# Splitting the first load of a 2x nearest-neighbour upsampling over two DMA queues

## The chip, the cores and the metric

The kernel runs on one core of a Trainium2 chip. The metric is the device time of one execution in microseconds, the median of several runs. The profile that is quoted below was taken on one execution; its times count from the core's first recorded instruction that is shown, here the first DMA issue.

## The reference

The input is an array of 16 x 64 images of 64 x 64 float32 values. Each pixel is repeated twice along each axis, so that the output has images of 128 x 128. Nothing is computed: the output is four copies of every input value, in order.

```python
batch, channels, h, w = (16, 64, 64, 64)
...
for i in range(new_h):
    for j in range(new_w):
        src_i = i // scale_factor
        src_j = j // scale_factor
        result[:, :, i, j] = x[:, :, src_i, src_j].copy()
```

The input is 16.78 MB and the output 67.11 MB.

## The kernel before

The 65,536 image rows are laid over 128 partitions, 512 consecutive rows (R = 512) of 64 values each, so that a partition owns one contiguous stretch of the input (128 KB) and one of the output (512 KB). A single on-chip tile, `mem`, holds both the input (`xt`, its upper part) and the expanded rows (`u`), which are written alternately at the bottom of the tile and downwards from the end of input rows that have been used up.

The loads are three DMAs at L195, cut by `cuts`: rows 0 to 32 (`HEAD`, 8 KB of every partition, 1.05 MB), rows 32 to 288 (64 KB of every partition, 8.39 MB) and rows 288 to 512 (56 KB, 7.34 MB). SyncE issues all three.

The work then goes through nine groups of rows (`rows = [54, 38, 54, 60, 54, 62, 64, 62, 64]`). For each group VectorE copies its rows from `xt` into `u` with a broadcast that repeats each value and each row (L215), and one DMA (L217) stores `u` to the output. Group 0 is copied in two instructions: its first row alone (L214), then the other 53 (L215), which need the second load, since group 0 ends at row 54. SyncE issues the stores of groups 0, 1 and 8, ScalarE those of groups 2 to 7. The profile shows one DMA queue for each of the two issuing engines.

The order of instructions comes from the program and from semaphores that the framework places. Two functions change it by hand when the program is finished. `begin_before_barrier` takes the first `EARLY = 3` instructions of SyncE out of the program's body and puts them ahead of the opening barrier, in front of SyncE's drain, so that the loads are issued before the engines have met. `close_early` rebuilds the end of the program: the closing barrier is passed while the last store is still under way, GpSimd clears the semaphores, and SyncE alone waits for the last landing.

Of the kernel before, what the change touches and what calls it, by code (L numbers as in the profile page):

```python
# [6 lines left out]

EARLY = 3  # L10


def begin_before_barrier(nc):

    blocks = nc.main_func.blocks
    main, body = blocks[0], blocks[1]
    sp = mybir.EngineType.SP
    loads = [i for i in body.instructions if i.engine == sp][:EARLY]  # L20
    for load in loads:
        assert isinstance(load, mybir.InstDMACopy), type(load)
        assert not (load.sync_info and load.sync_info.on_wait)
    names = [i.name for i in loads]
    body.instructions = [i for i in body.instructions if i.name not in names]
    kept = list(main.instructions)
    at = next(
        n
        for n, i in enumerate(kept)
        if i.engine == sp and isinstance(i, mybir.InstDrain)  # L30
    )
    kept[at:at] = loads
    main.instructions = kept


def close_on_gpsimd(nc):
# [117 lines left out]
@with_exitstack  # L154
def kernel(
    ctx: ExitStack,
    tc: tile.TileContext,
    x: bass.AP,
    scale_factor: int,
    out: bass.AP,  # L160
):
    nc = tc.nc
    nc.at_finalize(begin_before_barrier)
    nc.at_finalize(close_early)
    P = nc.NUM_PARTITIONS
    s = int(scale_factor)
    B, C, H, W = x.shape
    R = B * C * H // P
    fdt = x.dtype

    xp = x.rearrange("b c h w -> (b c h) w").rearrange("(p r) w -> p r w", p=P)
    op = out.rearrange("b c (h hd) w -> (b c h) (hd w)", hd=s).rearrange(
        "(p r) w -> p r w", p=P
    )

    rows = [54, 38, 54, 60, 54, 62, 64, 62, 64]
    GROW = s * s
    FREE = 79
    WF = FREE * GROW * W
    assert sum(rows) == R
    mem_pool = ctx.enter_context(tc.tile_pool(name="mem", bufs=1))
    mem = mem_pool.tile([P, WF + R * W], fdt, name="mem")
    xt = mem[:, WF:].rearrange("p (r w) -> p r w", r=R)

    HEAD = 32
    cuts = [0, HEAD, R // 2 + HEAD, R]
    for lo, hi in zip(cuts, cuts[1:]):
        nc.sync.dma_start(out=xt[:, lo:hi], in_=xp[:, lo:hi])  # L195

    def expanded(r0, r1):
        return (
            xt[:, r0:r1].unsqueeze(2).unsqueeze(4).to_broadcast([P, r1 - r0, s, W, s])
        )  # L200

    r0 = 0
    before = (0, 0)
    for n, k in enumerate(rows):
        size = k * GROW * W
        at = 0 if n % 2 == 0 else WF + r0 * W - size
        assert at >= before[1] or at + size <= before[0]
        before = (at, at + size)
        u = mem[:, at : at + size].rearrange(
            "p (k a w b) -> p k a w b", k=k, a=s, w=W  # L210
        )
        k0 = 1 if n == 0 else 0
        if k0:
            nc.vector.tensor_copy(out=u[:, :k0], in_=expanded(r0, r0 + k0))  # L214
        nc.vector.tensor_copy(out=u[:, k0:], in_=expanded(r0 + k0, r0 + k))  # L215
        issuer = nc.sync if n in (0, 1, len(rows) - 1) else nc.scalar
        issuer.dma_start(out=op[:, r0 : r0 + k, :], in_=u)  # L217
        r0 += k
# [35 lines left out]
```

## Time and profile before

| What | Value |
|---|---|
| median of 3 runs | 197.12 us (197.11 to 197.22) |
| profiled execution: span | 195.7 us |
| profiled execution: own time | not listed apart from its span; the runs' median lies 1.4 us above it |
| VectorE busy | 76.9 us (39%) |
| DMA traffic | 83.89 MB in 1728 packets, mean 429 GB/s |
| DMA queue of SyncE / of ScalarE, share of 16 engines | 44.3% / 55.0% |
| chain that ended last | DMA 61%, VectorE 24% |

The span runs from the first DMA issue to the last instruction, which waits for the last store's landing. The table's share of a queue is the time that its packets took, as a share of the 16 DMA engines' time over the span; the two together are over 99%. In the tables by stretch a packet's bytes and its time are booked where the packet begins, so a short stretch can show more than a DMA engine can move, and the stretch after it nothing.

### The profile page before, as it was taken

How to read it: one execution, taken by the hardware profiler on the slowest of the kernel's cores; microseconds unless marked ns; L12 is line 12 of the kernel's file. 1: busy time of each engine (PE TensorE's matmuls, PEld its weight loads, DVE VectorE, ACT ScalarE, POOL GpSimd, SP SyncE). 2: the span in 40 equal slices, each digit the busy share in tenths (PEclk: the TensorE clock that was granted, in tenths of full speed). 3: DMA queues.
4: the chain of work that ended last, by engine and by line, in shares of the span. 5: the costliest groups of instructions: out<-in, count | busy, mean ns of one | idle time of the engine just before them, and what ended most of it. 6: DMA issues, size and time to landing. Idle time of an engine off the chain costs nothing.

```text
span 195.7 us, 76 instructions
## 1 busy us (share of the span) xinstructions
DVE 76.9 (39%) x10; POOL 0.2 (0%) x4
## 2 busy tenths in 40 slices
DVE  0000099990029287059008805920790079000000
POOL 0000000000000000000000000000000000000000
DMA  9999989989898988999999899999999999999994
GB/s 429 429 429 429 402 375 492 445 362 543 362 435 382 540 384 362 543 402 402 402 492 452 362 543 415 415 415 415 429 429 429 429 415 441 550 476 422 429 429 214
DMA packets 1728, 83.89 MB, mean 429 GB/s; under 512 B 192, under 2 KB 192, under 8 KB 192
## 3 DMA queue, kind: packets, MB, share of 16 engines
q10 hardware_dynamic: 864, 46.66, 55.0%
q1 hardware_dynamic: 864, 37.22, 44.3%
HBM read 16.78 MB, written 67.11 MB: 429 GB/s over the span
## 4 chain that ended last, share of the span: by engine, by line
DMA 61%; DVE 24%; SPq 0%; issue 0%
DMA out_dram<-mem 49%; DVE mem L215 24%; DMA mem<-in_x_dram 12%; SPq L195 0%
## 5 line engine op out<-in xcount | busy, mean ns | idle before, releaser
L215 DVE COPY mem<-mem 128x13824 f32<-128x13824 f32 (+5 forms) x9 | 76.6, 8515 | 84.6 <-DMA out_dram<-mem 65.5
L214 DVE COPY mem<-mem 128x256 f32<-128x256 f32 x1 | 0.3, 293 | 4.9 <-DMA mem<-in_x_dram 4.9
L235 POOL MEMSET const-bfloat16-1.0<- 128x1 bf16 x1 | 0.1, 101 | 0.0
L235 POOL MEMSET const-uint8-127<- 128x1 uint8 x1 | 0.1, 101 | 0.0
L235 POOL MEMSET const-float32-0.0<- 128x1 f32 x1 | 0.1, 98 | 0.2 <-issue 0.2
L235 POOL MEMSET const-float32-1.0<- 128x1 f32 x1 | 0.1, 98 | 0.0
## 6 DMA issues: line engine op xcount, KB each, us to landing
out_dram<-mem ACTq DMA_DIRECT2D x2, 7936.0 KB, 31.6
out_dram<-mem ACTq DMA_DIRECT2D x2, 6912.0 KB, 23.7
out_dram<-mem ACTq DMA_DIRECT2D x1, 7680.0 KB, 26.1
mem<-in_x_dram SPq DMA_DIRECT2D x1, 7168.0 KB, 40.2
out_dram<-mem SPq DMA_DIRECT2D x1, 6912.0 KB, 18.9
out_dram<-mem SPq DMA_DIRECT2D x1, 4864.0 KB, 25.1
mem<-in_x_dram SPq DMA_DIRECT2D x1, 1024.0 KB, 4.8
mem<-in_x_dram SPq DMA_DIRECT2D x1, 23.8
```

Of the source, the lines that this page charges most:

```text
L214: nc.vector.tensor_copy(out=u[:, :k0], in_=expanded(r0, r0 + k0))
L215: nc.vector.tensor_copy(out=u[:, k0:], in_=expanded(r0 + k0, r0 + k))
L235: nc = _bacc.Bacc("TRN2", target_bir_lowering=False, num_devices=1)
```

## The change

The first of the three loads, rows 0 to 32 of all 128 partitions, is replaced by two: partitions 0 to 63 issued by SyncE and partitions 64 to 127 issued by ScalarE. The other two loads stay as they are, on SyncE. `EARLY` becomes a table, and `begin_before_barrier` does for each engine in it what it did for SyncE: three DMA issues of SyncE and one of ScalarE are put ahead of the opening barrier. The copy at L214 has two landings to wait for instead of one.

```diff
-EARLY = 3
+EARLY = {mybir.EngineType.SP: 3, mybir.EngineType.Activation: 1}
...
-    sp = mybir.EngineType.SP
-    loads = [i for i in body.instructions if i.engine == sp][:EARLY]
...
+    for engine, count in EARLY.items():
+        loads = [i for i in body.instructions if i.engine == engine][:count]
...
+        at = next(
+            n
+            for n, i in enumerate(kept)
+            if i.engine == engine and isinstance(i, mybir.InstDrain)
+        )
+        kept[at:at] = loads
+        main.instructions = kept
...
     HEAD = 32
     cuts = [0, HEAD, R // 2 + HEAD, R]
-    for lo, hi in zip(cuts, cuts[1:]):
+    half = P // 2
+    nc.scalar.dma_start(out=xt[half:, :HEAD], in_=xp[half:, :HEAD])
+    nc.sync.dma_start(out=xt[:half, :HEAD], in_=xp[:half, :HEAD])
+    for lo, hi in zip(cuts[1:], cuts[2:]):
         nc.sync.dma_start(out=xt[:, lo:hi], in_=xp[:, lo:hi])
```

More of the change, by code (lines that the diff above doesn't have):

```diff
@@ L18, in begin_before_barrier @@
     main, body = blocks[0], blocks[1]
-    sp = mybir.EngineType.SP
-    loads = [i for i in body.instructions if i.engine == sp][:EARLY]
[L21 to L33, printed above, removed]
+    for engine, count in EARLY.items():
+        loads = [i for i in body.instructions if i.engine == engine][:count]
+        for load in loads:
+            assert isinstance(load, mybir.InstDMACopy), type(load)
+            assert not (load.sync_info and load.sync_info.on_wait)
+        names = [i.name for i in loads]
+        body.instructions = [i for i in body.instructions if i.name not in names]
+        kept = list(main.instructions)
+        at = next(
[5 more added lines that the diff above has]
+        main.instructions = kept
 def close_on_gpsimd(nc):
```

## The prediction

> **What bounds the kernel now.** I read the page first: the span, the DMA strip and the traffic; then the chain that ended last; then tables of busy time by stretch.
>
> ```profile
> span 195.7 us, 76 instructions
> DMA  9999989989898988999999899999999999999994
> HBM read 16.78 MB, written 67.11 MB: 429 GB/s over the span
> DMA packets 1728, 83.89 MB, mean 429 GB/s; under 512 B 192, under 2 KB 192, under 8 KB 192
> L215 DVE COPY mem<-mem 128x13824 f32<-128x13824 f32 (+5 forms) x9 | 76.6, 8515 | 84.6 <-DMA out_dram<-mem 65.5 <-DMA mem<-in_x_dram 19.1
> L214 DVE COPY mem<-mem 128x256 f32<-128x256 f32 x1 | 0.3, 293 | 4.9 <-DMA mem<-in_x_dram 4.9
> ```
>
> The strip cuts the span into 40 slices, and the DMA engines are at eight or nine tenths in all but the last. 16.78 + 67.11 = 83.89 MB go through in 195.7 us. Two stretches of steady work, one of loads and one of stores, give the rate (columns: stretch, length, VectorE, GpSimd, clock, DMA share, GB/s):
>
> ```profile
> 5.00:24.00 19.00, 0.15 (x1) 0.00 (x0) 1.00 1.00 435
> 157.00:187.00 30.00, 8.69 (x1) 0.00 (x0) 1.00 1.02 441
> ```
>
> At 435 GB/s 83.89 MB last 192.9 us. So 195.7 - 192.9 = 2.8 us is all that the span holds beside a full stream: its start and its last landing. VectorE is busy for 76.9 us (76.6 + 0.3) and waits on DMAs for the rest, so it is not the bound; the chain's early steps show how the work hands over.
>
> ```profile
> 21 pieces in order of time: start us, us, what
> 0.00 0.37 SPq L195
> 0.37 0.05 issue
> 0.42 23.76 DMA mem<-in_x_dram
> 24.19 0.02 issue
> 24.21 14.30 DVE mem L215
> 38.51 0.02 issue
> 38.52 18.93 DMA out_dram<-mem
> ...
> ```
>
> The chain starts with the second load (23.76 us from its issue), not the first. The first store is issued at 38.52 and takes 18.93 us to land at 57.45. Its size and the loads' landings say whether the stream ran dry there:
>
> ```profile
> L195 SPq DMA_DIRECT2D mem<-in_x_dram x3: 373/424/432, 0.0 to 0.9; - x3
> DMA to landing us min/median/max: 4.8/23.8/40.2
> out_dram<-mem SPq DMA_DIRECT2D x1, 6912.0 KB, 18.9
> ```
>
> 6912 KB are 7.08 MB, or 16.3 us at 435 GB/s; counted back from 57.45 the store's bytes began at about 41.2. The third load, issued at 0.9, landed 40.2 us later, at 41.1. The store stood 2.6 us in the queue behind it and there was no hole. So whatever the DMA engines lose or gain in the first microseconds reaches the end in full, and nothing later takes it up or adds to it.
>
> **The first load, close up.** The first 5 us in 40 slices of 0.125 us: share of the DMA engines, and GB/s, where a packet's bytes stand where it begins. Below it, whole microseconds of the table by stretch.
>
> ```profile
> DMA  0000000099330023699999999999979999990000
> GB/s 0 0 0 0 0 0 0 0 393 590 66 66 0 0 66 131 262 393 393 393 459 459 393 459 393 393 459 393 524 328 393 524 852 2753 2622 2622 0 0 0 0
> ```
>
> ```profile
> 4.00:5.00 1.00, 0.14 (x1) 0.00 (x0) 1.00 2.56 1106
> 5.00:6.00 1.00, 0.15 (x1) 0.00 (x0) 1.00 0.00 0
> 6.00:7.00 1.00, 0.00 (x0) 0.00 (x0) 1.00 2.42 1049
> 7.00:8.00 1.00, 0.00 (x0) 0.00 (x0) 1.00 0.00 0
> 8.00:9.00 1.00, 0.00 (x0) 0.00 (x0) 1.00 0.30 131
> 9.00:10.00 1.00, 0.00 (x0) 0.00 (x0) 1.00 2.12 918
> ```
>
> Three things. First packets begin 1.0 us after the issue (eight empty slices), and the flow is steady from about slice 16, 2.0 us. From there 0.125 us carries about 410 GB/s until slice 32, where the large packets of the second load follow with no empty slice between: the handover from one DMA to the next costs nothing that can be seen. And the sixteen engines walk nearly in step: 1049 GB/s over 1 us is 1.05 MB, sixteen packets of 64 KB, that is one packet of every engine begun between 6 and 7 us, none between 5 and 6 or 7 and 8. The large packets first begin in four slices (852 to 2622), so the engines lie within 0.5 us of one another.
>
> **The change, part by part.** The load of 1.05 MB (128 partitions of 8 KB, eight packets an engine) becomes two of 0.52 MB. I assume that each spreads over all sixteen engines, four packets of 8 KB each.
>
> Issue. ScalarE gains one DMA issue, SyncE keeps three. Rows:
>
> ```profile
> L217 ACTq DMA_DIRECT2D out_dram<-mem x6: 338/339/376, 64.9 to 146.9; - x6
> L235 ACTq DRAIN x1: 8/8/8, 0.1 to 0.1; - x1
> L235 SPq DRAIN x1: 125/125/125, 1.4 to 1.4; - x1
> ```
>
> ScalarE reaches the barrier at 0.1 us and SyncE at 1.4, so ScalarE's 0.34 to 0.38 us are over by 0.5, a microsecond ahead of the barrier: no cost, and if that cover were gone VectorE still has nothing to do until 4.9. SyncE's first issue, 0.37 us for 128 partitions, may shrink; if it went by partitions the loads behind it would leave 0.19 us sooner. A sooner start is worth something only for the first packets: between 0 and -0.2; I take -0.1, the middle, since the 0.34 us store issue and the 0.37 us load issue differ little with size.
>
> Waits. The copy at L214 now waits for two landings. It is followed by 19 us of idle time before the large copy at L215, which hangs on the second load (24.21), so even a first load that lands at 12 us, its upper packets alternating with three 64 KB packets of 2.4 us, costs nothing. Completion marks: the 192 packets under 512 B are sixteen for each of the twelve DMAs, so a thirteenth adds sixteen; the slices around the handover put their price at 0. The later stores wait for one more semaphore that came 20 us earlier, and sit in a queue anyway (2.6 us at the tightest place worked out above): 0.
>
> The transfer itself. No row of this trace shows a transfer over 64 partitions. Bounds: if the sixteen engines are the limit, 1.05 MB last 2.41 us as now, change 0. If the side of the on-chip memory is the limit and 64 partitions give half of it, a stretch in which all engines are in one half goes at half rate: 4.82 us, +2.41. Loads and stores both run at 435 to 441 GB/s though one reads and the other writes the outer memory, so the limit is in what they share, engines or on-chip side; this does not tell which. I take the upper region, nearest to the in-step rows: SyncE's packets reach every engine first, ScalarE's come some 0.1 us behind, so all sixteen engines want the lower half at the same moment, then all the upper. It is not the whole 2.41, because engines that are apart miss each other. For two engines that share a way in, a packet of 0.30 us (2.41/8) takes 0.60 - d when they are d apart. Over a spread of 0.5 us two engines are 0.17 us apart on average: 8 x 0.13 = 1.0 us. But the end waits for the slowest engine, which is in one of the closest pairs; I choose d = 0.075, a quarter packet: 8 x 0.225 = 1.8 us.
>
> [...]
>
> Sum: -0.1 + 0 + 0 + 1.8 = +1.7 us. The profiled span of 195.7 becomes 197.4. The runs' median is 197.12, 1.4 above the span, for what lies around it and is not touched: 198.8.
>
> **Rivals.**
> (a) The halves cost nothing: the engines are the limit, or half of them are soon in the upper half while the others are in the lower. For it: after the start the spread (0.5 us) is more than a packet (0.30), so some pairs are out of step already. Against it: it needs all eight pairs out of step, as the slowest one sets the end. Price 0 to -0.2 from the issue and 0.2 of leftover collisions: 196.9 to 197.3, centre 197.0.
> (b) Faster: the two queues ramp up side by side. The strip shows 1.0 us from 1.0 to 2.0 in which sixteen first packets are on their way and little follows. If a second queue's packets travel in that time, a part is saved: at most 1.0 less one packet's own 0.30, 0.7 us, together with the -0.1 of the issue 196.3; half of it 196.7. It decides over (a) when over 0.3 us of the ramp goes, with no collision. Against it: after the ramp packets already flow at the full rate in a single queue, so their way is already overlapped, and a ramp that two queues share has the same first arrival.
> (c) The change does not do what it says: the upper half starves behind the second load. Then its four packets an engine are met by large packets of other engines, and both sides pay: up to 8 x 0.30 = 2.4 us, 199.5; more if the second load's landing slips past its cover of 1.6 us (2.6 in the queue less 1.0 from issue to first packet).
>
> **How the numbers follow.** Forecast, collisions with 0.9 to 2.5 us lost: 198.0 to 199.6, chance 0.62. Rival (a) 0.24. Rival (b) 0.10. Rival (c) with more than 2.5 us lost 0.04; its smaller losses are in the forecast. About 0.2%, 0.39 us, is what a measurement of this kernel can tell from no change: the forecast and (c) lie above it, (a) within, (b) below. So faster 0.10, same 0.24, slower 0.66. The time is that of the forecast, 198.8, whose own range is 198.0 to 199.6. It holds 0.62 alone, so the range reaches down over (a) to 196.9, and to 199.6 above: 0.86, with (b) and the rest of (c) left out.
>
> **What would show it.** Right: in the first 5 us the slices from 2.0 on carry well under 410 GB/s, some near 200; the large packets begin about 1.5 to 2.2 us later than slice 32 and spread over more than 0.5 us; the large copy at the second load's landing starts near 25.9 instead of 24.21, and all later copies are as late. ScalarE's load stands near 0.1 us and SyncE's first issue is 0.2 to 0.37 us. Wrong: the slices keep 410 GB/s and the large copy starts within 0.3 us of 24.21 (rival a), or sooner (b). A landing of the second load that is late while the end is not would overthrow the first part, that early losses reach the end in full.

## The result and the profile after

The changed kernel takes 199.58 us (199.45 to 199.68), before 197.12 us: ratio 1.0119, 95% interval 1.0107 to 1.0131. It is 2.46 us slower; 198.8 had been forecast. Run once more beside the last experiments it took 199.23 us against 197.20 (1.0100, 1.0086 to 1.0113), so the loss is 2.0 to 2.5 us.

The page of the changed kernel (VectorE's copies stand at L217 and L218 now):

```profile
span 198.2 us, 80 instructions
HBM read 16.78 MB, written 67.11 MB: 423 GB/s over the span
L218 DVE COPY mem<-mem 128x13824 f32<-128x13824 f32 (+5 forms) x9 | 76.6, 8515 | 84.4 <-DMA out_dram<-mem 65.5
L217 DVE COPY mem<-mem 128x256 f32<-128x256 f32 x1 | 0.3, 293 | 7.4 <-DMA mem<-in_x_dram 7.4
mem<-in_x_dram SPq DMA_DIRECT2D x1, 512.0 KB, 5.0
mem<-in_x_dram ACTq DMA_DIRECT2D x1, 512.0 KB, 7.3
```

The same bytes take 2.5 us longer. VectorE is as busy as before (76.6 + 0.3 us) and its idle time behind stores is the same 65.5 us. Only the loads' landings moved: the lower half needs 5.0 us from its issue, the upper 7.3, where the whole load had needed 4.8, and the two loads behind land later in turn (26.0 us instead of 23.8, 42.3 instead of 40.2). The chain of waits shows that the loss is complete at the second load's landing:

```profile
0.00 0.55 SPq L196
0.55 0.06 issue
0.60 26.00 DMA mem<-in_x_dram
26.60 0.02 issue
26.62 14.30 DVE mem L218
40.92 0.02 issue
40.94 18.92 DMA out_dram<-mem
59.85 0.02 issue
```

The large copy starts at 26.62 instead of 24.21 (+2.41), the first store is issued at 40.94 instead of 38.52 (+2.42) and has landed at 59.85 instead of 57.45 (+2.40). From there on nothing is made up; the span is 2.5 longer.

The first 5 us in slices of 0.125 us, with the DMA queues in that window below (packets, MB; q1 is SyncE's, q10 ScalarE's):

```profile
DMA  0000000000999010295699993669908599289936
GB/s 0 0 0 0 0 0 0 0 0 0 328 328 262 0 66 0 66 393 197 262 459 393 328 459 66 131 131 393 328 0 197 131 393 328 66 197 393 393 66 131
q1 hardware_dynamic: 80, 0.52, 46.1%
q10 hardware_dynamic: 41, 0.34, 29.2%
```

Ten empty slices instead of eight: the first packets come two slices later, at 1.32 us instead of 1.00 by the packet records of the trace, which have the start and the length of every DMA packet. Then, where before every slice from 2.0 on carried some 410 GB/s, bursts and gaps alternate, from 0 to 459 GB/s a slice: the packets begin in groups. SyncE's queue has begun 80 packets, the 64 of the lower half and their 16 completion marks, and nothing of the second load, though that was issued at 0.6; the upper half has begun 41. So the engines worked through the lower half, then the upper, then went on: by the packet records the lower half's last packet begins at 3.54 us, the upper half's begin from 3.45 to 5.88, and the second load's first at 5.80. The rate by stretches, before first and after second (DMA share, GB/s at the end of the row):

```profile
2.50:3.50 1.00, 0.00 (x0) 0.00 (x0) 1.00 1.00 426
```

```profile
2.50:5.50 3.00, 0.00 (x0) 0.00 (x0) 1.00 1.07 246
```

The engines are occupied throughout (share 1.00 and 1.07), but move 246 GB/s instead of 426.

### The profile page after: what moved, and what is told of

Same layout as the page of the kernel before. It is cut to its first block, busy times and chain, and to the rows that moved or that the text cites. A ratio compares the mean times of both kernels' runs of the same rounds, so it can differ in the third digit from the quotient of the medians.

```text
span 198.2 us, 80 instructions
## 1 busy us (share of the span) xinstructions
DVE 76.9 (39%) x10; POOL 0.2 (0%) x4
## 4 chain that ended last, share of the span: by engine, by line
DMA 61%; DVE 23%; SPq 0%; issue 0%
DMA out_dram<-mem 48%; DVE mem L218 23%; DMA mem<-in_x_dram 13%; SPq L196 0%
## 5 line engine op out<-in xcount | busy, mean ns | idle before, releaser
L218 DVE COPY mem<-mem 128x13824 f32<-128x13824 f32 (+5 forms) x9 | 76.6, 8515 | 84.4 <-DMA out_dram<-mem 65.5
L217 DVE COPY mem<-mem 128x256 f32<-128x256 f32 x1 | 0.3, 293 | 7.4 <-DMA mem<-in_x_dram 7.4
## 6 DMA issues: line engine op xcount, KB each, us to landing
mem<-in_x_dram SPq DMA_DIRECT2D x1, 7168.0 KB, 42.3
```

## The experiments

Theory "width" or "sides": a DMA into 64 neighbouring partitions is slow because all sixteen engines crowd into one half of the on-chip memory. Rivals: two queues that start side by side disturb each other; any DMA under 128 partitions is slow; a fixed cost of the extra DMA.

The edits are shown in part. They are made to the kernel before, but for "Two queues, split by rows instead of partitions" and "The change with quarters", which are made to the changed kernel. `EARLY` always follows the number of loads, so that all of them go out ahead of the barrier; it is shown in the first edit only.

**Both halves on one queue.**

```diff
-EARLY = 3
+EARLY = 4
...
+    half = P // 2
+    for p in (0, half):
+        nc.sync.dma_start(out=xt[p : p + half, :HEAD], in_=xp[p : p + half, :HEAD])
```

> Both halves of the first load on SyncE's queue, ScalarE issues none. Theory 'width' (a DMA over 64 partitions moves at half rate because all sixteen engines are in the same half at once): 8 KB packets of about 0.62 us, the large copy near 26.3 us, 199.2 to 199.6 us, as slow as the changed kernel but for its 0.3 us later first packets. Rival 'queues' (two queues that start together disturb each other): 0.31 us packets, large copy at 24.2, 197.1 us.

Measured 199.25 us, ratio 1.0104 (1.0089 to 1.0119): as slow as the change. Its stretch from 2.5 to 5.5 us, and its large copy in the chain of waits:

```profile
2.50:5.50 3.00, 0.00 (x0) 0.00 (x0) 1.00 1.05 227
```

```profile
26.33 14.30 DVE mem L218
```

ScalarE's queue isn't needed for the loss. My expectation that this form would have earlier first packets was wrong: the issue took 0.55 us here too.

**Two queues, split by rows instead of partitions.**

```diff
+    mid = HEAD // 2
+    nc.scalar.dma_start(out=xt[:, mid:HEAD], in_=xp[:, mid:HEAD])
+    nc.sync.dma_start(out=xt[:, :mid], in_=xp[:, :mid])
```

> The first load split by rows instead: rows 0 to 16 of all 128 partitions on SyncE, rows 16 to 32 on ScalarE, both ahead of the barrier. Theory 'width': 4 KB packets of about 0.15 us, full rate, 197.1 to 197.5 us (up to 0.3 us for two issues side by side). Rival 'queues': as slow as the changed kernel, 199.6 us.

Measured 197.32 us, ratio 1.0008 (0.9998 to 1.0017): no difference that can be measured. In the timeline the first landing even comes at 4.04 instead of 4.86, and the large copy does not move:

```profile
4.04 0.29 DVE L217 COPY mem<-mem 128x256 f32<-128x256 f32 x1 [4.04 <-DMA mem<-in_x_dram]
24.21 19.55 DVE L218 COPY mem<-mem 128x13568 f32<-128x13568 f32 x2 [19.88 <-DMA mem<-in_x_dram]
```

So two queues are harmless here, and a landing that is 0.8 us earlier is worth nothing here. The rival of the queues has fallen.

**Four DMAs of 32 partitions, one queue.**

```diff
+    part = P // 4
+    for p in range(0, P, part):
+        nc.sync.dma_start(out=xt[p : p + part, :HEAD], in_=xp[p : p + part, :HEAD])
```

> The first load in four DMAs of 32 partitions, all on SyncE. Theory 'width' by halves of the memory (32 partitions are as narrow as 64): packets of about 0.62 us, first load 4.8 us instead of 2.4, 199.2 to 199.8 us. Rival 'width in proportion' (the rate goes with the number of partitions): packets of 1.2 us, 9.6 us instead of 2.4, 204.3 us. Rival 'queues': 197.1 us.

Measured 198.89 us, ratio 1.0088 (1.0073 to 1.0103).

```profile
2.50:4.50 2.00, 0.00 (x0) 0.00 (x0) 1.00 1.02 229
```

32 partitions run at the rate of 64, 229 against 227 GB/s, not at half of it. The large copy starts at 26.19:

```profile
26.19 14.30 DVE mem L218
```

**The second load in halves.** The first load is whole; the 8.39 MB behind it go as partitions 0 to 63, then 64 to 127.

```diff
+    lo, hi = cuts[1], cuts[2]
+    for p in (0, half):
+        nc.sync.dma_start(out=xt[p : p + half, lo:hi], in_=xp[p : p + half, lo:hi])
```

> The first load whole as before; the second load (8.39 MB) in two DMAs of 64 partitions, both on SyncE. Theory 'width': 64 KB packets of 4.8 us instead of 2.4, eight an engine, +18.5 to +19.3 us: 215.6 to 216.4 us, the large copy near 43. Rival 'fixed cost of two more narrow DMAs' (+2.4 whatever the size): 199.5 us. Rival 'engines fall out of step and miss each other over a long transfer': between, about 205.

Measured 218.42 us, ratio 1.1080 (1.1063 to 1.1096).

```profile
10.00:40.00 30.00, 0.00 (x0) 0.00 (x0) 1.00 1.02 210
```

The loss grows with the bytes (+21.2 us) and a steady 210 GB/s stands where 435 stood, a little under half; hence more than the 18.5 to 19.3 expected. In the packet records the 64 KB packets of the two halves take about 5.12 us, where those of the whole load take 2.42. The rival of engines that fall out of step had put the total at about 205 us; over these 30 us the rate stays at 210 GB/s.

**Half the partitions, from both sides.** Partitions 32 to 95 in one DMA, then 0 to 31 and 96 to 127.

```diff
+    for p, q in ((32, 96), (0, 32), (96, 128)):
+        nc.sync.dma_start(out=xt[p:q, :HEAD], in_=xp[p:q, :HEAD])
```

> The first load as partitions 32 to 95 in one DMA (64 of them, half from below 64 and half from above), then 0 to 31, then 96 to 127, all on SyncE. Theory 'sides' (a packet is slow because all engines are on one side of partition 64 at once): the middle DMA's packets 0.31 us, those of the other two 0.62; the transfer 3.6 us instead of 2.4, and 0.3 us later first packets as the 64-partition issue of e1 showed: large copy near 25.5, 198.4 to 198.8 us. Rival 'any DMA under 128 partitions is slow': all packets 0.62 us, large copy near 26.3, 199.2 us.

Measured 198.97 us, ratio 1.0091 (1.0074 to 1.0108). The first stretch is the middle DMA, the second the outer ones:

```profile
2.30:3.30 1.00, 0.00 (x0) 0.00 (x0) 1.00 0.95 393
3.50:4.50 1.00, 0.00 (x0) 0.00 (x0) 1.00 1.12 262
```

This is the run that decides, by its rates: 64 partitions that straddle partition 64 move at 393 GB/s, 32 on one side at 262 in the stretch where the one DMA hands over to the other and on. In the packet records nearly all packets of the middle DMA begun between 2.5 and 3.0 us take 0.31 us, as those of a whole load do; from 3.6 us on packets take 0.52 to 0.61. So the slow packets here go not with the number of partitions (64 at 393 GB/s, 32 at 262) but with all of them lying on one side of partition 64. The total alone would not decide: 198.97 us lies above the 198.4 to 198.8 that were expected for this theory and below the rival's 199.2, and the large copy (25.88) lies between the two as well. Half of the bytes are still on one side at a time and the issue of this form is as long (0.61 us).

One rival is untested. A partition's number also sets its place in the outer memory, and no run moved the one without the other. The last store, in the next run, speaks against it: its partitions lie 512 KB apart there, those of the loads 128 KB, and its packets are as slow (5.11 us against 5.12 for 64 KB).

**The last store in halves, on two queues.**

```diff
+        if n == len(rows) - 1:
+            half = P // 2
+            nc.scalar.dma_start(out=op[half:, r0 : r0 + k, :], in_=u[half:])
+            nc.sync.dma_start(out=op[:half, r0 : r0 + k, :], in_=u[:half])
```

> Loads as before; the last store (8.39 MB) as two DMAs of 64 partitions, the lower on SyncE and the upper on ScalarE at the same moment. Theory 'sides': the engines walk in step, so two queues do not spread them over both sides, and a store suffers like a load: 19.3 us become some 39 to 41, 214 to 219 us. Rival 'two queues together fill both sides': 197.1 us. Rival 'only writes into the on-chip memory suffer': 197.1 us.

Measured 221.97 us (220.54 and 223.39), ratio 1.1254, slower than either expectation. A stretch of whole stores, one with both halves under way, and one with the upper half nearly alone:

```profile
150.00:165.00 15.00, 7.06 (x1) 0.00 (x0) 1.00 0.99 428
190.50:198.50 8.00, 0.00 (x0) 0.00 (x0) 1.00 1.02 279
200.00:206.00 6.00, 0.00 (x0) 0.00 (x0) 1.00 0.98 208
```

The store by halves is as slow as the loads by halves: the upper half nearly alone moves at 208 GB/s, and its 64 KB packets take 5.11 us there, as the halves of a load did. The two halves were hardly side by side: until about 190 us the upper one stood behind an earlier store of ScalarE, while the lower one shared the engines with that store. Where both halves were under way the rate was 279 GB/s, above the 208 of the upper half nearly alone and far from the 428 of whole stores, so two queues gave back only a part of the rate. At the end, from 211 to 217 us, the packet records have the engines busy for 0.47 of the time: some have finished while others still have packets, which goes with a total above the expectation.

**No separate first load.** Rows 0 to 288 as one DMA; the first row's copy is joined to the large one.

```diff
-    cuts = [0, HEAD, R // 2 + HEAD, R]
+    cuts = [0, R // 2 + HEAD, R]
...
-        k0 = 1 if n == 0 else 0
+        k0 = 0
```

> No separate first load: rows 0 to 288 in one DMA, two DMAs in all, the copy of row 0 joined to the large copy. If the end is set by the stream alone and the early landing serves nobody: 196.9 to 197.3 us, the large copy at 24.0 to 24.5. If the first landing matters after all: later by up to the 0.3 us of the small copy or more.

Measured 198.36 us, ratio 1.0056 (1.0041 to 1.0071): a miss. From the chain of waits and the DMA issues (us to landing):

```profile
24.35 7.37 DVE mem L215
31.73 0.02 issue
31.74 26.84 DMA out_dram<-mem
```

```profile
mem<-in_x_dram SPq DMA_DIRECT2D x1, 7168.0 KB, 41.8
```

Joined, the copy takes 7.37 us instead of 14.30, and the first store goes out at 31.74, while the third load is still running; that load then needs 41.8 us to land instead of 40.2. The delay is in its last packets, sixteen in each of these stretches, before and here:

```profile
38.15:40.30 2.15, 2.12 (x2) 0.00 (x0) 1.00 0.99 427
```

```profile
38.10:40.20 2.10, 0.00 (x0) 0.00 (x0) 1.00 1.53 437
```

They took 2.1 us each (0.99 x 2.15), and take 3.2 (1.53 x 2.10) with the first store waiting behind them. These 1.1 us are nearly all by which the span is longer (196.9 against 195.7); why the packets take longer is not shown. Two things had been changed at once, so the first landing's worth wasn't tested. The next run takes them apart.

**The same, with the two copies kept.**

```diff
-    cuts = [0, HEAD, R // 2 + HEAD, R]
+    cuts = [0, R // 2 + HEAD, R]
```

> No separate first load (rows 0 to 288 in one DMA), but the copies of group 0 in the two instructions of before, so that the first store is issued as late as before, near 38.8 us; e7 had joined the copies and its first store went out at 31.7, into the third load. If the early landing serves nobody and the loss of e7 came from its early store: 197.1 to 197.5 us. If the separate first load itself is worth something: 198.3 us as e7.

Measured 197.71 us, ratio 1.0024 (1.0015 to 1.0034). That is outside both expectations. By the medians the joined copy with its early store accounts for about half of the 1.1 us of the run before; in the profile the third load's last packets take 2.2 us again. The remaining 0.5 us isn't seen in the profiled execution, whose own time is 197.18 us at a span of 195.9, the fastest of the eleven; what it is stays open.

**Four DMAs of 16 partitions and one of 64.**

```diff
+    for p, q in ((0, 16), (16, 32), (32, 48), (48, 64), (64, 128)):
+        nc.sync.dma_start(out=xt[p:q, :HEAD], in_=xp[p:q, :HEAD])
```

> The first load as four DMAs of 16 partitions (0 to 63) and one of 64 (64 to 127), all on SyncE. Theory 'sides' alone (two sides, each half the rate): packets of 0.62 us throughout, as e3: 198.7 to 199.3 us. Rival 'finer ways in' (16 neighbouring partitions are a quarter of the ways in, half of what 32 have): packets of 1.2 us for the first four DMAs, 4 x 0.93 + 4 x 0.31 = 5.0 us lost: 201.5 to 202.3 us.

Measured 200.21 us, ratio 1.0151 (1.0131 to 1.0172), between both expectations.

```profile
2.50:4.50 2.00, 0.00 (x0) 0.00 (x0) 1.00 1.03 135
5.00:6.50 1.50, 0.00 (x0) 0.00 (x0) 1.00 1.02 218
```

16 neighbouring partitions move at 135 GB/s, 64 at 218 in the same run. Two sides alone would have left 16 partitions at the 229 GB/s of 32, and the rival's half of that, which was an assumption, would be 115; 135 lies between them. What sets it is not shown.

**The change with quarters.** Each engine issues its half as two DMAs of 32 partitions.

```diff
+    half, part = P // 2, P // 4
+    for p in (0, part):
+        q = half + p
+        nc.scalar.dma_start(out=xt[q : q + part, :HEAD], in_=xp[q : q + part, :HEAD])
+        nc.sync.dma_start(out=xt[p : p + part, :HEAD], in_=xp[p : p + part, :HEAD])
```

> As the change, but each engine issues its half as two DMAs of 32 partitions. If the 0.3 us later first packets of the changed kernel come from the 64-partition form of the DMA (issue 0.55 us instead of 0.38): first packets at 1.0, issue of 0.38 to 0.42 us, 0.3 us less than the changed kernel, 199.2 us. If they come from two queues starting side by side: no gain, 199.6 us.

Measured 198.66 us, ratio 1.0069 (1.0056 to 1.0082), 0.57 less than the changed kernel beside it, and below the 199.2 expected:

> The changed kernel once more beside the two others, for the 0.3 us between it and e1 and e10: 199.4 to 199.7 us.

which took 199.23 us, a little under its range. The issues of the quarters, and the large copy in the chain:

```profile
L198 SPq DMA_DIRECT2D mem<-in_x_dram x2: 386/398/409, 0.0 to 0.4; - x2
```

```profile
25.82 14.30 DVE mem L220
```

In the changed kernel's second profile:

```profile
26.34 14.30 DVE mem L218
```

With two queues and short issues the loss at the large copy is 1.61 us, against 2.13. The long issue (0.55 us, against 0.39 to 0.44 for these quarters) goes with the 64-partition form, not with two queues. How much of the 0.5 us between them is the issue stays open, since quarters on two queues also change the order of the packets (SyncE's two land 3.2 and 5.0 us after their issue, ScalarE's 4.2 and 6.0); on one queue, quarters gain 0.14 us over halves at the large copy (26.19 against 26.33).

## Why the prediction was right, and where its sizes were off

**Early losses reach the end in full:** held. +2.41 us at the large copy is +2.40 at the first store's landing and +2.5 at the end.

**The transfer, +1.8 us by half rate with the engines nearly in step:** right in kind and close in size. The packet records have the first load's packets from 1.00 to 4.49 us before, from 1.32 to 6.52 in the changed kernel and from 1.33 to 6.18 in its second profile: 1.7 and 1.4 us longer. The choice between the two bounds, taken from the in-step rows, is what the runs bore out: the rate goes to 229 GB/s with 32 partitions on a side and stays at 393, near the 426 of the whole load, with 64 across both. That 64 partitions on one side would have half the rate was an assumption; 246 GB/s stood where 426 had stood, and 210 where 435 had in the long transfer. That all engines went through the lower half before the upper was as assumed. The two engines that share a way in were the author's model, and no run shows such pairs; the quarter packet by which they were to miss each other was a choice, and no constant: once past the first packets, those of the lower half grow from 0.31 to about 0.63 us, and the last ones of the upper half take 0.62 to 0.65, a little over the 0.60 that the model had for a full collision. That the sum came so near is in part luck.

**The issue, -0.1 us:** this is a step that failed. It was reckoned that 64 partitions might be issued faster than 128, from the store and load issues. They are issued more slowly, outside the 0.2 to 0.37 us that were named as a sign of being right:

```profile
L196 SPq DMA_DIRECT2D mem<-in_x_dram x1: 547/547/547, 0.0 to 0.0; - x1
```

0.55 us instead of 0.37, with the first packets two slices later. In place of -0.1 stands +0.3 us at the first packet.

**The handover to the second load, not in the sum:** the prediction saw it cost nothing between whole loads. Behind halves it costs. These lines have the first sixteen packets of the second load, one of every engine; first the changed kernel (its 5.75 to 6.55 us), then the split by rows (3.88 to 4.45 us):

```profile
q1 hardware_dynamic: 16, 1.05, 354.1%
```

```profile
q1 hardware_dynamic: 16, 1.05, 424.6%
```

A packet takes 2.83 us (3.541 x 0.80) behind the halves and 2.42 (4.246 x 0.57) behind the rows. The packet records show a mean of 2.75 to 2.86 us for it in every run that split the first load by partitions. Whether these 0.4 us are the tail of the slow halves or a price of their own is not shown.

Together: 0.3 + 1.7 + 0.4 = 2.4 us, the +2.41 at the large copy; in the second profile 0.3 + 1.4 + 0.4 = 2.1, against 2.13. The forecast had 1.7. Its range still held, but only just: 199.58 us lies 0.02 below the upper end, and the room that was left for stronger collisions took up two terms that the sum did not have.

**Waits, marks, cover:** held. The small copy came at 7.42, far inside its cover of 19 us, and one more completion and wait cost nothing that shows.

**Rivals.** (a), halves at no cost, and (b), two queues ramping side by side, fell with the 246 GB/s; the split by rows shows what (a) would have looked like. (c), the upper half starving behind the second load, didn't happen: its packets went ahead of the second load's, and its 512 KB had landed at 7.4 (0.1 + 7.3).

## What to carry to other kernels

Where the DMA stream has no hole, as here, look for who waits for a landing before moving it earlier: a first landing 0.8 us sooner bought nothing. If a transfer is split, split it along the free dimension, as by rows here, and keep all 128 partitions in each part: by rows the same split over the same two queues cost nothing that could be measured (197.32 us against 197.19), by partitions it took the rate from 426 GB/s to 246. The loss by partitions showed in loads on one queue (227 GB/s) and on two, and in a store (208 GB/s where whole stores had 428); the split by rows was tried with a load only.

## What had not been expected

A DMA over 64 partitions takes 0.53 to 0.61 us to issue, and where it is the first its packets come 0.3 to 0.4 us later, while loads over 16, 32 and 128 partitions take 0.37 to 0.46 us unless they are issued right behind one of 64 (0.57 us in the changed kernel, up to 0.63); it does so on either side of partition 64, on SyncE and ScalarE, for loads and for the last store (0.53 and 0.54 us). The 64 partitions across the middle ran at 393 GB/s, nearly the 426 of the whole load. And a first store that goes out seven microseconds sooner (31.74 us instead of 38.52), while the loads still run, went with a kernel that is slower (198.36 us against 197.23), not faster. Nor had it been expected that the first packets of the whole load behind the halves would take 2.83 us instead of 2.42.
